# Operands' offsets in SBUF, the layout of the S5 kernel in memory, and the place of a root among GpSimd's tables

## The chip, the cores and the metric

The kernel runs on one core of a Trainium2 chip. The metric is the device time of one execution in microseconds. Inputs and outputs lie in DRAM; weights come as float32 and stay float32.

## The reference, cut to what matters

One decoder block on x of 512 tokens by 2048 channels:

```
mod = silu(c) @ w_ada + b_ada                 # 6 sections of 2048: sh1 sc1 ga1 sh2 sc2 ga2
h = rmsnorm(x, g) * (1 + sc1) + sh1
u, q, kc, vc, ks, vs, kw, vw, gl = split(h @ w_in)
y_ssm = S5(u)        # 64 groups of 16 channels, 64 complex states each; gelu and a gated 1024x1024 product
y_att = NSA(q, ...)  # 16 heads: compressed, selected and windowed attention, gated
x = x + ga1 * (concat(rmsnorm(y_ssm), rmsnorm(y_att)) @ w_out)
h = rmsnorm(x, g2) * (1 + sc2) + sh2
up = causal_conv3(h @ w_up) + conv_b          # 2048 -> 2 x 5632
x = x + ga2 * ((silu(gate) * val) @ w_down)
out = rmsnorm(x, g_final)
```

For S5, the states' decay `a = exp(lam * dt)` gives tables of powers of a for each group, with sines and cosines built by polynomials and angle doubling. S5 needs them, together with `f = (a - 1) / lam`.

## The kernel before

**Products.** Every float32 operand is split into a high part (a cast to a shorter float32, the type `fp32r` in the profile) on ScalarE (ACT) and a low part (source minus high part) on VectorE (DVE). `mm3` (L85 to L89) then makes three matmuls for each pair of tiles: wh·xh, wh·xl and wl·xh. In names such as `dn<-ah,wh` of the profile the first input (ah) streams through TensorE (PE) as the moving operand and the second (wh) is the 128x128 tile of weights. Each matmul loads its own weights.

**Stages**, in the order of time: phase A (0 to 240 us) makes the modulation and the first norm and projects u, k and v. Its first half multiplies by `wu` for u, its second half by `wk`. b1 (240 to 540) makes the 12 remaining projections and, between them, 8 octets of S5 (8 groups each), and ends with the gate and the compressed keys. b2 is attention with the gated product of S5 beside it, and c the output projection (together 540 to about 1033). Then the up projection (`up_first` for 2 of 44 channel blocks, `up_rest` for 42) until 1860, and the down projection until 2350, with the last norm behind it.

**Up projection.** `up_rest` makes each block by 7 products in place of 8 (a Strassen-like scheme): for 7 weight tiles (`a11`, `a12`, `a22`, and sums such as `a21 + a22`) and 7 operands of 256 columns that stand ready (`b11`, `b21`, `t4`, `t1`, `t2`, `b22`, `t3`, each with a part h and a part l). A product is 8 steps of `mm3`, so 24 matmuls of 256 columns, and a block is 168 matmuls. The split weights go in turn into the pair wh, wl of the pool `wp` and the pair xh, xl of the pool `pe` (L1167 to L1174), so that half of all products use each pair. `up_first` uses wh, wl and a pair rh, rl.

**Where the tiles lie.** Pools are opened like a stack from the left and, with `side="right"`, from the right of each partition's memory. A pad `rp` of 8 floats is the first on the right (L1314), and the tile `tapn` (with a pad to 48 x 3 floats, L1326) stands on the left ahead of everything opened after it. The pool `wp` stands ahead of both. The start addresses, modulo 128 bytes, of moving operand and weights are therefore, before the change:

```
matmuls                                        moving  weights
up, dn, mm (yh, yl), b1 and A with wh, wl        64       64
up with xh, xl and with rh, rl                   64        0
dn with wz (the last 96 of the down projection)  64        0
s<-K,Q (scores)                                   0        0
pv<-tl,Vs and pv<-th,Vs                          64        0
```

**First norm.** In phase A the sums of squares go through TensorE, DVE adds epsilon (`rms_v`, L131), GpSimd (POOL) takes the power -1/2 (`rms_r`, L133), and TensorE spreads the result (L136) for the scale `rb`, which the whole second half of phase A needs. GpSimd also computes the S5 tables (`s5_prep`, L325 to L481), in one instruction stream. The stream is written by a scheduler; `tc.high_priority(-100000)` puts the tables behind everything else, and a list `hold` binds two copies at the beginning of the second half of the tables to a place behind the root. Behind the tables stand the queue's DMA writes of k and v (`qk_d`, `v_d`).

**S5 in an octet** (L491 to L636). Tables of the octet on DVE (`s5C`, `s5S`, `s5bb`, `s5bg`, `s5TT`), weights `s5W` by transposes on TensorE, a product of `bb` and `TT` that gives the octet's convolution kernel `Kt` of 16 x 1024, its write to DRAM (`k_s`, L582), a read back as a banded 128 x 128 x 8 tile (`s5w3`, shown as `s5w` in the profile, L586), then states by a scan, and the output Y, to which 8 matmuls with `w3[:, :, g]` as weights (L631) and 8 with `TT` (L632) contribute. `Kt`, `k_s` and `w3` have the group index g innermost, so that the 128 weights of one group lie 32 bytes apart. Octets are issued in the loop over the projections (L706).

Of the kernel before, what the change touches and what calls it, by code (L numbers as in the profile page):

```python
# [18 lines left out]
P = 128  # L19
# [28 lines left out]
M_K, M_C = 0, 512  # L48
NM = 640


class Block:
# [88 lines left out]
    def setup(self):  # L141
# [3 lines left out]
        self.dp = ctx.enter_context(tc.tile_pool(name="dp", bufs=1, space=DRAM))  # L145
        cp = self.cp

        self.vecs = cp.tile([P, 176], F32, name="vecs")[:, 0:NV]
# [48 lines left out]
    def phase_a(self, hh, hl, tab, ps):  # L197
# [4 lines left out]
        with ExitStack() as st:  # L202
# [59 lines left out]
            for kt in range(KT):  # L262
# [12 lines left out]
                if kt == 1:  # L275

                    zero = pa.tile([P, P], F32, name="zero")
                    nc.gpsimd.memset(zero, 0.0)
                    self.after([nc.gpsimd.dma_start(
                        self.k_s.rearrange("o i x -> (o i) x")[:, 1024:].rearrange("p (a b) -> p a b", b=P),  # L280
                        zero.unsqueeze(1).to_broadcast([P, 7, P]))], first)
                if 2 <= kt < 10:
# [42 lines left out]
    def s5_prep(self, pool, W):  # L325
        nc, tc, V = self.nc, self.tc, self.nc.gpsimd
        sgn, nsgn = self.cst(C_SGN), self.cst(C_NSGN)
        vin = W.tile([P, 3, 64], F32, name="vin")
        nc.sync.dma_start(vin, self.a["s5v"])
        with tc.high_priority(-100000):  # L330
# [79 lines left out]

            for m in (1, 2, 4):
                cmul(PR[:, 8 - 2 * m:8 - m], PI[:, 8 - 2 * m:8 - m], PR[:, 8 - m:8], PI[:, 8 - m:8],
                     bc(PR[:, 8 - m], m), bc(PI[:, 8 - m], m), tmp[:, :m])
            ar, ai = PR[:, 7], PI[:, 7]
            den, q, rd, nr = t(), t(), t(), t()
# [30 lines left out]
            def powers(C, Sn, c, s):  # L446
                V.memset(C[:, 0], 1.0)
                V.memset(Sn[:, 0], 0.0)
                after = [V.tensor_copy(C[:, 1], c), V.tensor_copy(Sn[:, 1], s)]
                if hold:  # L450
                    self.after(after, hold.pop())
                cmul(C[:, 2], Sn[:, 2], C[:, 1], Sn[:, 1], C[:, 1], Sn[:, 1], tmp[:, 0])
                cmul(C[:, 3], Sn[:, 3], C[:, 2], Sn[:, 2], C[:, 1], Sn[:, 1], tmp[:, 0])
                ec, es = t(), t()
                cmul(ec, es, C[:, 2], Sn[:, 2], C[:, 2], Sn[:, 2], tmp[:, 0])
                cmul(C[:, 4:8], Sn[:, 4:8], C[:, 0:4], Sn[:, 0:4], bc(ec, 4), bc(es, 4), tmp[:, :4])
                return ec, es

        yield

        hold = [self.rms_pow]
        with tc.high_priority(-100000):
            ec, es = powers(CB, SB, c8, s8)
# [27 lines left out]
    def s5_octet(self, o, Tb, W, ps):  # L491
# [78 lines left out]
        Kt = W.tile([P, 8, 9 * 16], F32, name="s5bg", bufs=3).rearrange("p a b -> p (a b)")  # L570
        Kt = Kt[:16, 0:1024].rearrange("p (x g) -> p x g", g=8)
        with hp():
            for q in range(2):
                p = ps.tile([P, 4, P], F32, name="tp", bufs=2)
                for g in range(4):
                    T.matmul(p[:16, g], bb[:, 0, 4 * q + g], TT[:, 4 * q + g, 1:9].rearrange("p k h -> p (k h)"),
                             start=True, stop=True)
                A.copy(Kt[:, :, 4 * q:4 * q + 4].rearrange("p x g -> p g x"), p[:16])
        dd = W.tile([16, 16, 8], F32, name="s5dd")
        nc.sync.dma_start(dd, a["s5d"][:, o])  # L580
        V.tensor_add(Kt[:, 112:], Kt[:, 112:], dd)
        nc.gpsimd.dma_start(self.k_s[o, :, 0:1024].rearrange("i (x g) -> i x g", g=8), Kt)  # L582
        w3 = W.tile([P, P, 8], F32, name="s5w3")

        src = self.k_s[o]
        nc.gpsimd.dma_start(w3.rearrange("p x g -> p (x g)"),  # L586
                            bass.AP(src.tensor, src.offset, [[P, 8], [15 * P, 16], [1, 1024]]))

# [39 lines left out]
        with hp():  # L628
            Y = ps.tile([P, S], F32, name="acc", bufs=4)
            for g in range(8):  # L630
                T.matmul(Y[:, 64 * g:64 * g + 64], w3[:, :, g], U[:, g], start=True, stop=False)  # L631
                T.matmul(Y[:, 64 * g:64 * g + 64], TT[:, g, 0:8].rearrange("p k h -> p (k h)"), SS[:, g, 0:64],  # L632
                         start=False, stop=True)
            zz = W.tile([P, 8, 64], F32, name="s5x", bufs=4)
            A.activation(zz.rearrange("p g j -> p (g j)"), Y, AF.Gelu_apprx_tanh)
            nc.gpsimd.dma_start(self.z_d[o].rearrange("(h g) l j -> l h g j", g=8), zz)  # L636
# [24 lines left out]
    def phase_b1(self, hh, hl):  # L661
        nc, tc, a, V, A, T = self.nc, self.tc, self.a, self.V, self.A, self.T
        with ExitStack() as st:
# [17 lines left out]
            for i in range(12):  # L681
# [3 lines left out]
                with tc.high_priority():  # L685
# [13 lines left out]
                    else:  # L699
# [5 lines left out]
                        self.spill(self.qk_d[g, P * t:P * t + P], p, t2, -0.125)  # L705
                while 12 * n < 7 * (i + 1):  # L706
                    octet(n)
                    n += 1
# [602 lines left out]
    def run(self):  # L1311
        tc = self.tc
        self.setup()
        self.ctx.enter_context(tc.tile_pool(name="rp", bufs=1, side="right")).tile([P, 8], F32, name="pad")  # L1314
        sc = ExitStack()
# [9 lines left out]
        self.taps = ta.tile([P, 88, 4], F32, name="taps")  # L1325
        self.tapn = ta.tile([P, NFF + 4, 3], F32, name="tapn")[:, 0:NFF]  # L1326
        with ExitStack() as st:
# [163 lines left out]
```

## Time and profile before

| | |
|---|---|
| times of three runs, us | 2372.95, 2373.53, 2375.1 (median 2373.53) |
| the profiled execution, us | 2375.8, span 2374.0 |
| granted TensorE clock, mean over the span | 0.964 |
| busy share of the span: PE, DVE, ACT, POOL | 94%, 79%, 46%, 12% |

The span is the time from the first to the last recorded instruction. "Busy" counts the time in which an engine had an instruction; matmuls overlap, so a busy TensorE can still be at different paces, and the distance between starts tells the pace. A granted clock of 1.0 is 2.4 GHz, 0.5 is 1.2 GHz.

### The profile page before, as it was taken

Reading aid. Unit: us, or ns where it says so; the run is one execution under the profiler, and the core shown is the slowest. Engines: PE = TensorE matmul, PEld = TensorE weight load, DVE = VectorE, ACT = ScalarE, POOL = GpSimd, SP = SyncE. Lnnn points to the kernel's source line nnn. Section 1 sums busy time; section 2 is a strip of 40 time slices with the busy share of each in tenths; the row PEclk is TensorE's granted clock in tenths of the full one; section 3 lists DMA queues with packets and bytes.
Section 4 is the critical chain, followed back from the end, with each engine's and each line's share of the span. In section 5 each row is a group of like instructions: output and inputs, shape, how many; then the busy total and the mean of one; then the engine's idle time right before and its main releaser. Section 6 shows DMA issues by size and latency. Waiting matters only on the chain.

```text
span 2374.0 us, 34691 instructions
## 1 busy us (share of the span) xinstructions
PE 2223.8 (94%) x13694; PEld 1963.5 (83%) x13694; DVE 1864.5 (79%) x2776; ACT 1083.3 (46%) x1807; POOL 284.5 (12%) x375
## 2 busy tenths in 40 slices
PE   7779999988899889899999999999999899999997
PEld 5657787866677667889999999999999788888887
DVE  7789878749988878889999999999999686434436
ACT  4222535448867742644444444444444422222215
POOL 7996110100000001000000000000000000000000
PEclk9889989979999889999999999999999999999998
DMA  8666745676567568233333333333333585333323
GB/s 342 257 218 224 238 143 148 186 207 193 183 215 228 185 251 302 99 123 119 117 117 120 118 117 118 118 118 118 118 118 120 233 313 227 124 107 124 107 89 107
DMA packets 92370, 398.17 MB, mean 168 GB/s; under 512 B 19776, under 2 KB 28352, under 8 KB 56240
## 3 DMA queue, kind: packets, MB, share of 16 engines
q1 hardware_dynamic: 77856, 344.60, 41.7%
q0 software_dynamic: 14352, 51.36, 6.3%
q8 instruction: 107, 1.75, 0.3%
q14 instruction: 55, 0.45, 0.1%
HBM read 358.20 MB, written 37.69 MB: 167 GB/s over the span
## 4 chain that ended last, share of the span: by engine, by line
PE 71%; DVE 10%; issue 6%; POOL 5%; ACT 4%; DMA 3%; SPq 0%; POOLq 0%; DVEq 0%; ACTq 0%
PE dn L88 7%; PE dn L87 7%; PE dn L89 7%; PE sa L89 7%; PE sa L88 7%; PE sa L87 7%; PE sb L87 5%; PE sb L89 5%; PE sb L88 5%; PE mm L87 2%; PE mm L89 2%; PE mm L88 2%; POOL stt L339 2%; DVE wl L62 2%; PE s L871 1%
## 5 line engine op out<-in xcount | busy, mean ns | idle before, releaser
L62 ACT CAST wh<-wr 128x1024 fp32r<-128x1024 f32 (+1 forms) x257 | 262.1, 1025 | 508.7 <-PE dn L88 324.3
L62 DVE TENSOR_TENSOR wl<-wr,wh 128x1024 fp32r<-128x1024 f32 (+1 forms) x255 | 307.2, 1209 | 64.2 <-ACT wh L62 43.2
L87 PE MATMUL dn<-ah,wh 128*128 128x512 f32 (+1 forms) x704 | 271.3, 386 | 7.5 <-ACT ah L62 7.5
L88 PE MATMUL dn<-al,wh 128*128 128x512 f32 (+1 forms) x704 | 271.3, 386 | 0.0
L89 PE MATMUL dn<-ah,wl 128*128 128x512 f32 (+1 forms) x704 | 271.0, 385 | 0.0
L1250 DVE SCALAR_TENSOR_TENSOR x<-dn,mod,x 128x512 f32<-128x512 f32 (+1 forms) x104 | 73.3, 709 | 192.4 <-PE dn L89 191.9
L87 PEld LDWEIGHTS dn<-ah,wh 128*128 128x128 f32 x704 | 132.8, 189 | 34.3 <-ACT ah L62 7.7
L111 DVE SCALAR_TENSOR_TENSOR adw<-adw,silc 128x2048 f32<-128x2048 f32 x63 | 150.2, 2386 | 11.8 <-DMA adw<-in_wada_dram 11.8
L88 PEld LDWEIGHTS dn<-al,wh 128*128 128x128 f32 x704 | 132.6, 188 | 26.9 <-DVE al L62 0.7
L89 PEld LDWEIGHTS dn<-ah,wl 128*128 128x128 f32 x704 | 132.7, 188 | 26.2
L62 ACT CAST wh<-wq 128x1024 fp32r<-128x1024 f32 x84 | 88.1, 1050 | 137.6 <-DVE wq L1194 101.1
L62 ACT CAST xh<-wq 128x1024 fp32r<-128x1024 f32 x84 | 87.9, 1046 | 135.9 <-DVE wq L1194 100.7
L87 PE MATMUL mm<-yh,wh 128*128 128x512 f32 (+1 forms) x320 | 129.4, 409 | 21.4 <-ACT yh L62 6.2
L88 PE MATMUL mm<-yl,wh 128*128 128x512 f32 (+1 forms) x320 | 128.3, 401 | 3.7 <-DVE yl L62 3.7
L1083 POOL DMA_DIRECT2D a_d<-cv x44 | 23.8, 541 | 877.4 <-DVE cv L1082 877.4
L62 DVE TENSOR_TENSOR wl<-wq,wh 128x1024 fp32r<-128x1024 f32 x84 | 102.4, 1220 | 32.9 <-ACT wh L62 32.9
L89 PE MATMUL mm<-yh,wl 128*128 128x512 f32 (+1 forms) x320 | 127.4, 400 | 0.4 <-DVE wl L62 0.4
L62 DVE TENSOR_TENSOR xl<-wq,xh 128x1024 fp32r<-128x1024 f32 x84 | 102.6, 1221 | 31.5 <-ACT xh L62 31.5
L1194 DVE TENSOR_TENSOR wq<-wq,wr 128x1024 f32<-128x1024 f32 x84 | 102.2, 1216 | 0.1
L87 PEld LDWEIGHTS mm<-yh,wh 128*128 128x128 f32 x320 | 63.0, 199 | 36.1 <-issue 11.6
L87 PE MATMUL b<-hh,wh 128*128 128x512 f32 x192 | 68.8, 416 | 23.5 <-ACT hh L239 14.7
L62 ACT CAST xh<-wr 128x1024 fp32r<-128x1024 f32 x63 | 65.8, 1045 | 44.8 <-PE sa L88 31.6
(525 smaller groups left out, 7210.5 us busy)
## 6 DMA issues: line engine op xcount, KB each, us to landing
adw<-in_wada_dram SPq DMA_DIRECT2D x49, 1024.0 KB, 6.7
wr<-in_wup_dram SPq DMA_DIRECT2D x46, 1024.0 KB, 4.9
wq<-in_wup_dram SPq DMA_DIRECT2D x42, 1024.0 KB, 6.8
wr<-in_wdn_dram SPq DMA_DIRECT2D x40, 1024.0 KB, 4.9
wr<-in_wada_dram SPq DMA_DIRECT2D x32, 1024.0 KB, 4.9
wr<-in_wout_dram SPq DMA_DIRECT2D x16, 1024.0 KB, 5.4
adw<-in_wada_dram POOLq DMA_DIRECT2D x14, 1024.0 KB, 6.9
wr<-in_wp_dram SPq DMA_DIRECT2D x12, 1024.0 KB, 5.3
```

The costliest lines, as they stand in the source:

```text
L62: return self.A.copy(hi, src), self.V.tensor_sub(lo, src, hi.bitcast(F32))
L87: self.T.matmul(ps, wh, xh, start=start, stop=False)
L88: self.T.matmul(ps, wh, xl, start=False, stop=False)
L89: self.T.matmul(ps, wl, xh, start=False, stop=stop)
L111: self.V.scalar_tensor_tensor(t, t, 1.0, self.silc, op0=ALU.mult, op1=ALU.mult, accum_out=out)
L339: V.tensor_scalar(w, x, c, None, op0=op0)
L871: T.matmul(s[:, :c + n], q[hd], K[b][:, i, k0:k0 + c + n], start=i == 0, stop=i == 1)
L1083: self.nc.gpsimd.dma_start(self.a_d[:, m], val)
L1194: V.tensor_add(src, src, add)
L1250: V.scalar_tensor_tensor(x, p, self.mod[:, 5, m:m + 1], x, op0=ALU.mult, op1=ALU.add)
```

## The change

It has four parts.

1. The pad `rp` grows from 8 to 24 floats, and `tapn` takes 160 floats in place of 144. Every tile on the right moves by 64 bytes modulo 128, and so does every tile on the left that is opened after `tapn`. The addresses are then: up, dn and mm with wh, wl: moving 0, weights 64. Up with xh, xl and rh, rl, and dn with wz: moving 0, weights 64. Scores 64, 64. pv with th, tl: 0, 64. Phase A and b1 stay at 64, 64.
2. The S5 kernel lies by group: `Kt`, `k_s` and `w3` have the group outermost, and `w3[:, g]` is contiguous. Rows of `k_s` are 8 pieces of 240 floats (128 of data, 112 zeros). Its write becomes 128 pieces of 512 bytes for each octet (16 of 4 KB before), its read 1024 pieces of 512 bytes (128 of 4 KB before).
3. The load of `vin`, from which the tables start, moves from the queue of SP to the head of GpSimd's. The first part of the tables ends after the first squaring, and everything from `square(2)` on is held behind the root.
4. Octets are issued by `12 * n < 8 * (i - 1)` in place of `12 * n < 7 * (i + 1)`.

```diff
+class Held:
+    def __init__(self, engine, hold):
+        self.engine, self.hold = engine, hold
+    def __getattr__(self, name):
+        def issue(*args, **kw):
+            i = getattr(self.engine, name)(*args, **kw)
+            self.hold(i)
+            return i
+        return issue
...
-                    zero = pa.tile([P, P], F32, name="zero")
+                    zero = pa.tile([P, 112], F32, name="zero")
...
-                        self.k_s.rearrange("o i x -> (o i) x")[:, 1024:].rearrange("p (a b) -> p a b", b=P),
-                        zero.unsqueeze(1).to_broadcast([P, 7, P]))], first)
+                        self.k_s.rearrange("o i (g x) -> (o i) g x", g=8)[:, :, P:],
+                        zero.unsqueeze(1).to_broadcast([P, 8, 112]))], first)
...
-        nc.sync.dma_start(vin, self.a["s5v"])
+        nc.gpsimd.dma_start(vin, self.a["s5v"])
...
-            for m in (1, 2, 4):
+            def square(m):
                 cmul(PR[:, 8 - 2 * m:8 - m], PI[:, 8 - 2 * m:8 - m], PR[:, 8 - m:8], PI[:, 8 - m:8],
                      bc(PR[:, 8 - m], m), bc(PI[:, 8 - m], m), tmp[:, :m])
+            square(1)
+        yield
+        V = Held(V, lambda i: self.after([i], self.rms_pow))
+        with tc.high_priority(-100000):
+            square(2)
+            square(4)
...
-                after = [V.tensor_copy(C[:, 1], c), V.tensor_copy(Sn[:, 1], s)]
-                if hold:
-                    self.after(after, hold.pop())
+                V.tensor_copy(C[:, 1], c)
+                V.tensor_copy(Sn[:, 1], s)
...
-        yield
-        hold = [self.rms_pow]
-        with tc.high_priority(-100000):
...
-        Kt = Kt[:16, 0:1024].rearrange("p (x g) -> p x g", g=8)
+        Kt = Kt[:16, 0:1024].rearrange("p (g x) -> p g x", g=8)
...
-                A.copy(Kt[:, :, 4 * q:4 * q + 4].rearrange("p x g -> p g x"), p[:16])
+                A.copy(Kt[:, 4 * q:4 * q + 4], p[:16])
...
-        nc.gpsimd.dma_start(self.k_s[o, :, 0:1024].rearrange("i (x g) -> i x g", g=8), Kt)
-        w3 = W.tile([P, P, 8], F32, name="s5w3")
+        nc.gpsimd.dma_start(self.k_s[o].rearrange("i (g x) -> i g x", g=8)[:, :, 0:P], Kt)
+        w3 = W.tile([P, 8, P], F32, name="s5w3")
...
-                            bass.AP(src.tensor, src.offset, [[P, 8], [15 * P, 16], [1, 1024]]))
+        nc.gpsimd.dma_start(w3, bass.AP(src.tensor, src.offset, [[16, 8], [15 * P, 16], [15 * 16, 8], [1, P]]))
...
-                T.matmul(Y[:, 64 * g:64 * g + 64], w3[:, :, g], U[:, g], start=True, stop=False)
+                T.matmul(Y[:, 64 * g:64 * g + 64], w3[:, g], U[:, g], start=True, stop=False)
...
-                while 12 * n < 7 * (i + 1):
+                while 12 * n < 8 * (i - 1):
...
-        self.ctx.enter_context(tc.tile_pool(name="rp", bufs=1, side="right")).tile([P, 8], F32, name="pad")
+        self.ctx.enter_context(tc.tile_pool(name="rp", bufs=1, side="right")).tile([P, 24], F32, name="pad")
...
-        self.tapn = ta.tile([P, NFF + 4, 3], F32, name="tapn")[:, 0:NFF]
+        self.tapn = ta.tile([P, 160], F32, name="tapn")[:, 0:3 * NFF].rearrange("p (c j) -> p c j", j=3)
```

The order of GpSimd's instructions around the root, of the kernel before (L133 is the root; `sp` and `stt` are temporaries of the tables, `s5CB` and `s5SB` tables of cosines and sines):

```order
L383 TENSOR_SCALAR dw<-sp_392 128x64
L339 TENSOR_SCALAR stt<-sp_391 128x64
L340 TENSOR_TENSOR sp_401<-stt,dw 128x64
L339 TENSOR_SCALAR stt<-sp_391 128x64
L340 TENSOR_TENSOR sp_402<-stt,sp_391 128x64
L444 TENSOR_SCALAR sp_416<-sp_402 128x64
L279 DMA k_s<-zero 128x7x128
L133 TENSOR_TENSOR rms_r<-rms_v,mhalf 128x4
L449 COPY s5CB<-sp_416 128x64
L449 COPY s5SB<-sp_401 128x64
L401 TENSOR_TENSOR s5CB<-s5CB 128x64
```

And of the changed kernel (its line numbers are higher by 13 to 17; L146 is the root, and a held instruction has L59, the line of the wrapper):

```order
L418 TENSOR_TENSOR s5PI<-s5PR,s5PI 128x64
L417 TENSOR_TENSOR s5PR<-s5PR,sp_331 128x64
L419 TENSOR_TENSOR sp_331<-s5PI,s5PR 128x64
L420 TENSOR_TENSOR s5PI<-s5PI,sp_331 128x64
L293 DMA k_s<-zero 1024x1x112
L146 TENSOR_TENSOR rms_r<-rms_v,mhalf 128x4
L59 TENSOR_TENSOR s5PR<-s5PR 128x128
L59 TENSOR_TENSOR sp_331<-s5PI 128x128
L59 TENSOR_TENSOR s5PI<-s5PR,s5PI 128x128
```

The root stood at place 154 of GpSimd's order and now stands at 107. 48 instructions that stood ahead of it are behind it now, and the load of `vin` came in ahead.

The end of the tables on GpSimd before:

```order
L476 TENSOR_SCALAR sp_413<-sp_413,cons 128x512
L479 COPY s5CH<-sp_412 64x256
L478 COPY s5SH<-sp_413 64x256
L479 COPY s5SH<-sp_413 64x256
L659 DMA qk_d<-adw 128x1024 x2
L305 DMA v_d<-adw 128x512
L659 DMA qk_d<-adw 128x1024 x2
L305 DMA v_d<-adw 128x512 x3
```

and now:

```order
L59 COPY s5CH<-sp_1059 64x256
L59 COPY s5SH<-sp_1060 64x256 x2
L59 TENSOR_TENSOR s5fr<-s5fr,sp_1005 128x64
L59 TENSOR_TENSOR s5fi<-s5fi,sp_1005 128x64
L59 TENSOR_SCALAR s5fi<-s5fi,cons 128x64
L675 DMA qk_d<-adw 128x1024 x2
L319 DMA v_d<-adw 128x512
L675 DMA qk_d<-adw 128x1024 x2
L319 DMA v_d<-adw 128x512 x3
```

The DMA writes of k and v stand right behind the last table in both; what stands ahead of the tables' end is longer by the instructions that were moved.

On TensorE, ACT, DVE and SP the order of b1 is the same, but for the reciprocal of the tables on DVE (from place 11 to the middle of phase A's second half) and for octets 6 and 7. The front of octet 6 on TensorE before, between the matmuls of a projection (`mm<-hh`) and ahead of the output of octet 5 (`acc<-s5U,s5w`):

```order
L568 MATMUL tp<-cons,s5bg 128x128 x8
L88 MATMUL mm<-hl_1512,wh 128x512
L89 MATMUL mm<-hh_106,wl 128x512
L87 MATMUL mm<-hh_108,wh 128x512
L88 MATMUL mm<-hl_1553,wh 128x512
L89 MATMUL mm<-hh_108,wl 128x512
L87 MATMUL mm<-hh_110,wh 128x512
L88 MATMUL mm<-hl_1594,wh 128x512
L622 MATMUL acc<-s5x,cons 128x512
L631 MATMUL acc<-s5U,s5w_3262 128x64
L89 MATMUL mm<-hh_110,wl 128x512
L576 MATMUL tp<-s5TT,s5bb 16x128 x8
```

and now, in the projection that follows the output of octet 5:

```order
L102 MATMUL mm<-hh_94,wl 128x512
L100 MATMUL mm<-hh_96,wh 128x512
L101 MATMUL mm<-hl_97,wh 128x512
L796 MATMUL tp<-qt 128x124
L585 MATMUL tp<-cons,s5bg 128x128 x4
L102 MATMUL mm<-hh_96,wl 128x512
L100 MATMUL mm<-hh_98,wh 128x512
L101 MATMUL mm<-hl_99,wh 128x512
L618 MATMUL acc<-bg,cons 128x8
L585 MATMUL tp<-cons,s5bg 128x128
L593 MATMUL tp<-s5TT,s5bb 16x128 x3
L625 MATMUL acc<-s5U,s5W_3600 128x64 x2
```

Transposes (`tp<-cons,s5bg`) and kernel products (`tp<-s5TT,s5bb`) of octet 6 moved behind the whole output of octet 5, and stand now among the sums of the octet's own input (`acc<-s5U,s5W`).

## Rows read from the trace of the kernel before

**Rows 1.** Busy time of the engines by stage. Columns: stretch in us, length, and for PE, PE's weight loads (PEld), DVE, ACT and POOL the busy us and in brackets the instructions; then the granted clock, the share of DMA and GB/s.

```profile
0.00:103.00 103.00, 88.25 (x379) 71.22 (x380) 85.42 (x112) 41.25 (x49) 84.63 (x101) 1.00 0.90 341
103.00:128.00 25.00, 3.21 (x13) 2.68 (x13) 2.37 (x3) 1.07 (x2) 24.20 (x63) 0.54 0.12 38
128.00:240.00 112.00, 99.03 (x397) 78.34 (x397) 103.78 (x104) 30.88 (x39) 86.58 (x67) 0.94 0.69 230
240.00:540.00 300.00, 282.74 (x1389) 233.02 (x1387) 224.40 (x419) 142.90 (x305) 31.29 (x47) 0.93 0.62 185
540.00:1120.00 580.00, 517.45 (x2980) 432.90 (x2981) 501.54 (x1061) 363.39 (x820) 35.33 (x58) 0.94 0.55 189
1120.00:1860.00 740.00, 739.84 (x6249) 732.71 (x6248) 677.77 (x745) 356.50 (x411) 19.97 (x37) 1.00 0.33 118
1860.00:2350.00 490.00, 482.50 (x2216) 402.62 (x2215) 254.59 (x307) 140.09 (x172) 1.08 (x2) 0.99 0.44 162
```

**Rows 2.** DVE's instructions in order of time, around the first norm. Columns: start us, length us, engine, line, operation, tiles and shapes; in square brackets the idle time before it and what ended it.

```profile
103.08 0.16 DVE L131 TENSOR_SCALAR rms_v<-b 128x4 f32<-128x4 f32 x1 [1.10 <-PE b L129]
...
128.14 0.94 DVE L310 SCALAR_TENSOR_TENSOR modt<-x,mod,rb 128x512 f32<-128x512 f32 x1 [22.69 <-ACT rb L258]
```

**Rows 3.** GpSimd's instructions in order of time (columns as in rows 2): the first table row, the last of the first squaring, and the root.

```profile
12.61 0.65 POOL L348 TENSOR_SCALAR ex<-vin 128x64 f32<-128x64 f32 x1 [11.16 <-DMA vin<-in_s5v_dram]
...
110.38 0.32 POOL L406 TENSOR_TENSOR s5PI<-s5PI,sp 128x64 f32<-128x64 f32 x1
...
123.04 1.22 POOL L279 DMA_DIRECT2D k_s<-zero  x1
124.29 1.06 POOL L133 TENSOR_TENSOR rms_r<-rms_v,mhalf 128x4 f32<-128x4 f32 x1
```

**Rows 4.** GpSimd's groups by line and shape from 105 to 123 us, where DVE is idle. Columns: line, operation, tiles, shapes, count, then busy us and mean ns, then idle us.

```profile
L340 POOL TENSOR_TENSOR sp<-stt,sp 128x64 f32<-128x64 f32 x4 | 1.3, 316 | 0.2
...
L403 POOL TENSOR_TENSOR s5PR<-s5PR,sp 128x256 f32<-128x256 f32 x1 | 0.7, 719 | 0.0
```

**Rows 5.** The same from 128 to 217 us, where DVE is busy.

```profile
L403 POOL TENSOR_TENSOR sp<-sp,sp 128x64 f32<-128x64 f32 x5 | 5.7, 1150 | 0.2
...
L403 POOL TENSOR_TENSOR s5CB<-s5CB,sp 128x256 f32<-128x256 f32 x1 | 2.8, 2789 | 0.0
```

**Rows 6.** GpSimd in order of time: the last tables and the first writes of k.

```profile
207.55 2.24 POOL L475 TENSOR_TENSOR sp<-sp,sp 128x512 f32<-128x512 f32 x1
...
215.18 0.89 POOL L479 COPY s5SH<-sp 64x256 f32<-64x256 f32 x1
239.25 0.68 POOL L659 DMA_DIRECT2D qk_d<-adw  x1 [23.18 <-DVE adw L62]
```

**Rows 7.** DVE in order of time at octet 0: the first uses of the tables, and the low part of the weights for the next projection.

```profile
243.54 0.62 DVE L546 TENSOR_TENSOR s5C<-s5CH,s5CB 128x256 f32<-128x256 f32 x1
...
244.58 0.62 DVE L547 TENSOR_TENSOR s5x<-s5SH,s5SB 128x256 f32<-128x256 f32 x1 [0.42 <-DMA qk_d<-adw]
...
246.56 1.22 DVE L62 TENSOR_TENSOR wl<-wr,wh 128x1024 fp32r<-128x1024 f32 x1
```

**Rows 8.** Weight loads on TensorE from 240 to 545 us, by line and shape: the strided `s5w` and contiguous ones. A float32 matmul loads its weights twice, so 128 loads are 64 matmuls.

```profile
L631 PEld LDWEIGHTS acc<-s5U,s5w 128*128 128x128 f32 x128 | 36.0, 323 | 3.5 <-issue 2.7
L632 PEld LDWEIGHTS acc<-s5SS,s5TT 128*128 128x128 f32 x128 | 21.3, 204 | 1.1 <-DVE s5SS L627 0.9
```

**Rows 9.** DMA issues: size of one and the median us from issue to landing.

```profile
s5w<-k_s POOLq DMA_DIRECT2D x8, 512.0 KB, 7.6
...
z_d<-s5x POOLq DMA_DIRECT2D x8, 256.0 KB, 6.3
```

**Rows 10.** All instructions with the tile `s5w`. Columns: line, engine, operation, tiles, count, then ns min/median/max, then the start of the first and the last in us.

```profile
L631 PEld LDWEIGHTS acc<-s5U,s5w x128: 312/314/338, 291.6 to 507.3; 128*128 128x128 f32 x128
...
L586 POOL DMA_DIRECT2D s5w<-k_s x8: 612/724/825, 277.4 to 479.8; - x8
```

**Rows 11.** TensorE in order of time in `up_rest`: the first matmul of three products that follow one another, each of 24 matmuls.

```profile
1399.27 0.28 PE L87 MATMUL sa<-t1h,xh 128*128 128x256 f32 x1
...
1401.99 0.28 PE L87 MATMUL sb<-t2h,wh 128*128 128x256 f32 x1
...
1404.87 0.28 PE L87 MATMUL sa<-b22h,xh 128*128 128x256 f32 x1
```

**Rows 12.** TensorE's groups in the down projection (1875 to 2350 us) by line and shape, those of 256 columns.

```profile
L88 PE MATMUL dn<-al,wh 128*128 128x256 f32 x25 | 7.1, 283 | 0.0
L89 PE MATMUL dn<-ah,wz 128*128 128x256 f32 x16 | 4.4, 276 | 0.0
```

**Rows 13.** TensorE in order of time in the down projection: the first and the ninth of 9 matmuls of 512 columns.

```profile
1999.72 0.39 PE L89 MATMUL dn<-ah,wl 128*128 128x512 f32 x1
...
2001.53 0.39 PE L88 MATMUL dn<-al,wh 128*128 128x512 f32 x1
```

**Rows 14.** TensorE in order of time in attention: the first and the fourth of 4 matmuls of 512 columns.

```profile
772.84 0.39 PE L907 MATMUL pv<-tl,Vs 128*64 128x512 f32 x1
...
773.52 0.39 PE L908 MATMUL pv<-th,Vs 128*128 128x512 f32 x1
```

**Rows 15.** TensorE in order of time in attention: two score matmuls of 256 columns and what follows them.

```profile
714.97 0.40 PE L871 MATMUL s<-K,Q 128*128 128x256 f32 x2
715.22 0.39 PE L88 MATMUL mm<-yl,wh 128*128 128x512 f32 x1
```

More of the change, by code (lines that the diff above doesn't have):

```diff
@@ L577, in s5_octet @@
                              start=True, stop=True)
-                A.copy(Kt[:, :, 4 * q:4 * q + 4].rearrange("p x g -> p g x"), p[:16])
+                A.copy(Kt[:, 4 * q:4 * q + 4], p[:16])
         dd = W.tile([16, 16, 8], F32, name="s5dd")
         nc.sync.dma_start(dd, a["s5d"][:, o])
-        V.tensor_add(Kt[:, 112:], Kt[:, 112:], dd)
-        nc.gpsimd.dma_start(self.k_s[o, :, 0:1024].rearrange("i (x g) -> i x g", g=8), Kt)
-        w3 = W.tile([P, P, 8], F32, name="s5w3")
+        V.tensor_add(Kt[:, :, 112:], Kt[:, :, 112:], dd.rearrange("p x g -> p g x"))
+        nc.gpsimd.dma_start(self.k_s[o].rearrange("i (g x) -> i g x", g=8)[:, :, 0:P], Kt)
+        w3 = W.tile([P, 8, P], F32, name="s5w3")
         src = self.k_s[o]
-        nc.gpsimd.dma_start(w3.rearrange("p x g -> p (x g)"),
-                            bass.AP(src.tensor, src.offset, [[P, 8], [15 * P, 16], [1, 1024]]))
+        nc.gpsimd.dma_start(w3, bass.AP(src.tensor, src.offset, [[16, 8], [15 * P, 16], [15 * 16, 8], [1, P]]))
         bu = W.tile([P, 2], F32, name="bu", bufs=2)
```

## The prediction

> **What bounds the kernel now.** I read the table by stage first [rows 1]. From 1120 to 1860 us TensorE is busy for 739.84 of 740 us at full clock, and DVE for 677.77: the up projection is set by the pace of its matmuls. In the down projection TensorE has 482.50 of 490 and DVE half. In b1 (240 to 540) TensorE has 282.74 of 300, DVE 224.40. So in these three stages a matmul that becomes shorter is worth nearly its saving. The odd stretch is 103 to 128: all engines but GpSimd stand still (TensorE 3.21 of 25 us).
>
> The order of time on DVE tells why [rows 2]: epsilon is added at 103.08, and a later instruction starts at 128.14 after 22.69 us of idling, released by the scale `rb`. On GpSimd [rows 3] the root, ready since 103.24, begins at 124.29, because the tables stand ahead of it. So about 22 us there are one wait for a queue.
>
> **Part 3, root and tables.** First the root's new time. The last row of the first squaring began at 110.38 [rows 3]; now only `k_s<-zero` (1.22 us) stands between it and the root. The tables began at 12.61, when `vin` had landed, after 11.16 us of idling; with the load at the head of GpSimd's queue and a flight of some 4 us I put the start at 5, so 7.6 earlier. Some held rows among those before 110.38 go too (about 2 us), but those that ran while DVE stood still now meet a busy DVE: a row of 64 columns takes 316 ns beside an idle DVE [rows 4] and 1150 beside a busy one [rows 5], which gives back some 3 us. 110.7 - 7.6 - 2 + 3 + 1.2 = 105, end 106, against 125.35. The second half of phase A so starts some 19 us earlier: the stall shrinks from 22 us to 3.
>
> Second, what is late next: the tables. 76 instructions stood behind the root and took 125.3 to 216.1 [rows 3, 6]; now there are 48 more by the order: 32 of 64 columns, 4 memsets, 6 of 128 and 6 of 256 columns. Beside a busy DVE I take 1.0, 0.2, 1.5 and 2.2 us (somewhat under the 1150 and 2789 ns of [rows 5], since not every row meets DVE), together 55. From 106 that makes 106 + 55 + 91 = 252. DVE reaches its first table use, L546, at 243.54 [rows 7], now 19 earlier, at 224.5, and stops. The last 27.5 us then run beside an idle DVE; by the rows of 512 columns (2.24 [rows 6] against about 1.4, twice the 719 ns of 256 columns [rows 4]) this is some 15 us. The tables end near 239.5. Behind them stand the writes of k, first issued at 239.25 before [rows 6], for which DVE's next instruction L547 waits until 244.58 [rows 7]. Now they are issued at 239.5, and L547 comes at about the same time as before. Behind it in DVE's order is the low part of the next projection's weights, made at 246.56 to 247.78 [rows 7]. TensorE's projection 0 moves up by the 19 us and is done long before; it waits there for some 16. So of 19 us saved about 3 are left at the end, and a restart after a long wait costs: behind the stall of before the granted clock of the stretch was 0.54 [rows 1]. I take -1.5 us. The load of `vin` itself costs nothing: GpSimd idled then for 11.16 us [rows 3], and SP's queue loses an issue. The reciprocal of the tables, now among DVE's rows of the second half, uses a sum that stands 10 rows behind the root; DVE comes to it some 40 us later, so it waits for nothing. If the tables ran that late, DVE's whole queue would stand behind it. Bounds: -19 (the tables end in time), +6 (the tables end 9 us later than worked out).
>
> **Part 2, the S5 kernel by group.** A strided weight load takes 323 ns, contiguous ones of the same shape 204 [rows 8]. 128 loads x (323 - 204) = 15.2 us over the octets, on an engine that is busy 94% of b1 [rows 1]. Against it: the read of 512 KB now consists of 1024 pieces of 512 bytes. Before it landed in 7.6 us; `z_d`, 1024 pieces of 256 bytes, in 6.3 [rows 9]. I expect 7 to 12, and the first read was issued at 277.4 for a first use at 291.6 [rows 10], so nothing; without that lead the output would wait for up to the 5 us more. ACT's copies of `Kt` and DVE's sum change only their strides, on engines with idle time in b1 [rows 1]. Part 4 leaves TensorE's order alone up to octet 6; there the front moves behind the output of octet 5, so the last two octets have fewer projection matmuls to hide DVE's tables. I take +4 for this, and -11 for parts 2 and 4 together; bounds 0 (the tail eats it all) and -24 (with some of the clock regained that b1 lacks, granted 0.93 [rows 1]).
>
> **Part 1, 64 bytes.** In `up_rest` all matmuls have one shape, and two weight pairs take turns. 24 matmuls with xh, xl take 1401.99 - 1399.27 = 2.72 us (113.3 ns each), the next 24 with wh, wl 1404.87 - 1401.99 = 2.88 (120.0) [rows 11]. The same in the down projection: 283 and 276 ns for wh and wz [rows 12]. By the table of addresses, the slow pair lies at the moving operand's address modulo 128, the fast one 64 bytes from it. After the change all up products are 64 apart, with the roles turned round (moving 0, weights 64), which no row shows. I take the distance as what matters: 42 blocks x 84 slow matmuls x 6.67 ns = 23.5 us, and 192 in `up_first`, 1.3. DVE with 678 of 740 us [rows 1] still has room when a block falls from 19.6 to 19.0 us.
>
> For 512 columns the down projection has 8 distances in 1.81 us, 226 ns, at distance 0 [rows 13]; pv, 64 apart, has 3 in 0.68, 227 [rows 14]. So I take nothing for the 2016 matmuls of 512 columns in the down projection and 864 of the output products. The bound is 6.67 ns each, -13.4 and -5.8. The 288 of 256 columns there give -1.9. Scores stay at distance 0.
>
> A rule speaks against this part. The Trainium skill, page "SBUF — State Buffer", section "Who interferes with whom", gives TensorE two read ports for the moving operand and for weights, independent of each other, and says that it never waits on anyone. By that rule alone the sum would lose all 26.7 us of part 1, and the time be 2361. The trace does not agree with it as it stands: 113.3 and 120.0 ns for one shape [rows 11]. It could be kept if the address of the weights alone decides, which is a rival.
>
> **Sum.** -1.5 - 11 - 24.8 - 1.9 = -39.2. From the profiled 2375.8 this is 2336.6. That execution lies 2.3 us above the median of 2373.53, so 2334.
>
> **Rivals.**
> - *512 columns gain too.* Both widths lose time at the weight load, which is equally long for either. For it: 226 ns is 13 more than 512 columns at 2.4 GHz need, as 120 is 13 more than 256 need. Against it pv's 227 [rows 14]. 2334 - 19 = 2315. Chance 17%.
> - *The stall's gain is kept.* The tables end by 224, as their rows are slowed less than I take. Against it the 2.8 us of [rows 5]. 2334 - 17 = 2317. 8%.
> - *The offset does nothing for up* (something else differs between the pairs, as the pool). 2334 + 26.7 = 2361. 8%.
> - *The tables end after 247, and b1 gains nothing,* because DVE's late work sets its end. 2334 + 6.5 + 1 + 11, about 2352. 5%.
> - *The slower one: the weights' own address decides.* Weights at 0 modulo 128 would be the quick ones, and all move to 64. Then xh, xl, rh, rl and wz fall to 120 ns: 3528 x 6.67 = 23.5, + 1.3 + 0.6 = +25.4, with -12.5 of parts 2 to 4: 2373.5 + 12.9 = 2386. It decides as soon as it outweighs 12.5 us, that is from about half of its price. For it: no row has moving 0 and weights 64. Against it: scores, with both at 0, take 0.25 us for two of 256 columns [rows 15], 125 each, not 113. 12%.
>
> **How the numbers follow.** The forecast, 2318 to 2350 on its own, has 50%. The range for 8 in 10 reaches from 2300 (the first two rivals in part together) to 2364 (the third inside); it leaves out the slower one and a few per cent at each end. A measurement of this kernel can tell 0.2% (4.7 us) from no change. Faster than that: forecast 50, the first two 25, most of the third and fourth 11, less a little for gains that cancel: 84%. Same: 5%. Slower: 11%, nearly all of the last.
>
> **What would show it.** In the profile after: a root soon after 105 us with a stall of about 3; L546 of octet 0 waiting for GpSimd for some 15 us, and TensorE idle ahead of projection 1; weight loads of `s5w` near 200 ns; 2.72 us for 24 matmuls in `up_rest` whichever pair, at full clock, and a stage that is 23 us shorter; 226 ns still in the down projection. I am wrong in direction if 24 matmuls take 2.88 us for both pairs, and in size if 512 columns fall to 220 ns or the tables hold nobody up.

## The result and the profile after

The changed kernel takes 2357.75 us in the median of 4 runs (2354.28 to 2360.18), the kernel before 2373.24 beside it: a ratio of 0.9932, 95% interval 0.9915 to 0.995. That is 15.5 us (12 to 20 by the interval), where 39 were forecast. The direction was right, the range held the time, and the size was wrong by more than half.

By stage, in the columns of [rows 1]:

```profile
103.00:128.00 25.00, 21.32 (x90) 16.90 (x90) 20.86 (x22) 8.69 (x13) 24.32 (x23) 0.93 0.66 198
128.00:240.00 112.00, 88.96 (x374) 70.57 (x373) 87.30 (x104) 31.89 (x41) 105.46 (x114) 0.92 0.67 233
240.00:540.00 300.00, 265.76 (x1395) 213.59 (x1394) 229.22 (x449) 135.64 (x313) 32.50 (x38) 0.93 0.64 181
540.00:1120.00 580.00, 513.73 (x2994) 428.25 (x2993) 497.53 (x1028) 357.96 (x804) 35.65 (x59) 0.94 0.54 187
```

Fixed windows mislead here, as the stages have moved. More is seen in the start of the first matmul of each stage, taken from the profiles of all kernels of this study. For the kernel before it is the time in us from the span's start, for the others the difference from it; "S5" is the first and the last matmul with `s5w` as weights.

```
                     norm  proj 0  S5 first  S5 last  scores  pv last  up_rest    down     end
before              125.4   239.6     292.0    507.3   512.5    855.2   1025.5  1875.8  2374.0
changed             -18.7   -29.2     -10.9    -15.1   -18.9    -11.2     -5.6   -28.9   -15.6
e1 offsets            0.8     0.1       0.5      2.0     1.9     -3.5     -4.3   -28.0   -15.4
e2 root             -18.7   -28.7     -12.4    -11.3   -11.4    -14.6    -15.7   -16.3   -15.0
e3 by group           0.2    -1.0       0.1    -20.8   -21.5    -23.8    -21.0   -20.8   -20.9
e4 octets             0.2     0.1      -0.2      9.8     6.1      8.3      6.9     7.4     6.9
e8 all but octets   -18.7   -29.3     -11.1    -32.6   -33.3    -32.1    -29.3   -53.0   -40.2
e10 all but offsets -18.8   -27.7     -11.3    -17.5   -21.3    -19.5    -16.7   -17.1   -16.9
e9 offset for up    -18.9   -29.2     -10.8    -31.2   -31.5    -35.0    -32.0   -55.6   -55.9
e6 weights at 0       0.4     1.0       1.4     -0.4    -0.5      0.5     -3.8   -27.0   -14.8
e11 writes of k     -18.8   -29.8     -20.7    -42.0   -31.8    -35.6    -37.4   -59.7   -58.7
e12 octets earlier  -18.3   -28.9      -8.6    -25.8    -5.7    -13.0    -15.2   -38.6   -39.0
e13 vin on SP       -14.4   -22.8      -6.9    -28.8   -29.0    -30.2    -27.6   -50.9   -51.1
e14 e11+e12         -18.9   -29.5     -20.9    -33.1   -12.4    -21.0    -20.7   -43.8   -44.2
```

The line of the changed kernel tells the story: 29 us ahead at projection 0, 11 at the first octet; 19 at the scores, 6 at `up_rest`; 29 again at the down projection, and 16 at the end. So something is given back in three places.

**The stall.** GpSimd and DVE in order of time (columns as in [rows 2]); they answer to [rows 2, 3, 6, 7]:

```profile
103.69 3.01 POOL L146 TENSOR_TENSOR rms_r<-rms_v,mhalf 128x4 f32<-128x4 f32 x1 [1.48 <-DVE rms_v L144]
231.50 1.21 POOL L675 DMA_DIRECT2D qk_d<-adw  x2
```

```profile
109.38 1.06 DVE L324 SCALAR_TENSOR_TENSOR modt<-x,mod,rb 128x512 f32<-128x512 f32 x1 [3.58 <-ACT rb L272]
229.94 0.61 DVE L563 TENSOR_TENSOR s5C<-s5CH,s5CB 128x256 f32<-128x256 f32 x1 [13.29 <-POOL s5SH L59]
236.17 0.60 DVE L564 TENSOR_TENSOR s5x<-s5SH,s5SB 128x256 f32<-128x256 f32 x1 [5.62 <-DMA qk_d<-adw]
238.03 1.24 DVE L75 TENSOR_TENSOR wl<-wr,wh 128x1024 fp32r<-128x1024 f32 x1
```

The root now waits 1.48 us for epsilon, where it stood behind the tables for 21 us before; DVE's idle time falls from 22.69 us to 3.58. The wait comes back at octet 0: 13.29 us for the tables and 5.62 for the writes of k behind them.

**TensorE's own waits** from 205 to 500 us, the longest (who waited for whom: us in total, times, longest):

```profile
PE mm L102 <- DVE wl L75: 17.5, 1, 17.5
PE acc L647 <- DMA s5w<-k_s: 7.3, 1, 7.3
```

The first is the price of the tables. The second is new: the output of the seventh octet (octet 6 of the order lists) waits for its kernel to come back from DRAM. The read of that kernel and its first use, in the changed kernel and then in e8 below, which differs from it by part 4 alone:

```profile
444.39 1.33 POOL L603 DMA_DIRECT2D s5w<-k_s  x1 [6.25 <-PE tp L585]
452.58 0.69 PE L647 MATMUL acc<-s5U,s5w 128*128 128x64 f32 x2 [7.29 <-DMA s5w<-k_s]
```

```profile
419.32 1.37 POOL L603 DMA_DIRECT2D s5w<-k_s  x1
440.40 0.33 PE L647 MATMUL acc<-s5U,s5w 128*128 128x64 f32 x2
```

With part 4 the read is issued at 444.39 us and TensorE is ready for it at 445.3, so it waits; without part 4 the read is issued 21 us ahead of its use. Two stretches of the changed kernel, the second half of phase A and the one around that wait, in the columns of [rows 1]:

```profile
106.70:210.30 103.60, 97.10 (x404) 77.15 (x405) 95.69 (x105) 31.35 (x38) 101.44 (x103) 0.97 0.74 249
443.20:497.40 54.20, 37.69 (x202) 29.27 (x200) 22.31 (x48) 17.70 (x39) 6.33 (x6) 0.80 0.63 135
```

The kernel before has this for the first of them:

```profile
125.40:239.60 114.20, 101.23 (x405) 80.51 (x406) 103.78 (x104) 30.96 (x39) 88.77 (x77) 0.92 0.69 228
```

The same work takes 10.6 us less, with 8.1 us less busy time of DVE and a granted clock of 0.97 in place of 0.92. In the stretch around the wait TensorE is busy for 37.69 of 54.20 us, at 0.80.

**Pace.** In `up_rest` 24 matmuls take 2.72 us now with either pair: 1397.20 - 1394.48 below, with xh and xl, and the median distance between starts with wh, wl is 113 ns too, against 120 in [rows 11]. In the down projection 8 distances are 1.87 us, 234 ns, against 1.81 in [rows 13].

```profile
1394.48 0.28 PE L100 MATMUL sb<-b11h,xh 128*128 128x256 f32 x1
...
1397.20 0.28 PE L100 MATMUL sa<-t4h,xh 128*128 128x256 f32 x1
```

```profile
1999.61 0.39 PE L100 MATMUL dn<-ah,wh 128*128 128x512 f32 x1
...
2001.48 0.39 PE L102 MATMUL dn<-ah,wl 128*128 128x512 f32 x1
```

So the offset sped up the matmuls of 256 columns and slowed those of 512.

### The profile page after: what moved, and what is told of

The parts are those of the page before. It is cut to its first block, busy times and chain, and to the rows that moved or that the text cites. A ratio compares the mean times of both kernels' runs of the same rounds, so it can differ in the third digit from the quotient of the medians.

```text
span 2358.4 us, 34686 instructions
## 1 busy us (share of the span) xinstructions
PE 2195.3 (93%) x13694; PEld 1917.5 (81%) x13694; DVE 1856.5 (79%) x2776; ACT 1074.7 (46%) x1807; POOL 310.3 (13%) x376
## 3 DMA queue, kind: packets, MB, share of 16 engines
HBM read 358.20 MB, written 37.69 MB: 168 GB/s over the span
## 4 chain that ended last, share of the span: by engine, by line
PE 57%; issue 4%; DVE 1%; ACT 1%; POOL 1%; DMA 1%; POOLq 0%; DVEq 0%; ACTq 0%
PE sa L102 7%; PE sa L100 7%; PE sa L101 7%; PE dn L100 7%; PE dn L101 7%; PE dn L102 7%; PE sb L100 5%; PE sb L102 5%; PE sb L101 5%; DMA adw<-in_wada_dram 0%; POOL adw L119 0%; DMA ar<-a_d 0%; POOL x_d L1045 0%; PE mm L100 0%; PE mm L101 0%
## 5 line engine op out<-in xcount | busy, mean ns | idle before, releaser
L75 ACT CAST wh<-wr 128x1024 fp32r<-128x1024 f32 (+1 forms) x257 | 262.0, 1024 | 521.9 <-PE dn L101 331.6
L146 POOL TENSOR_TENSOR rms_r<-rms_v,mhalf 128x2 f32<-128x2 f32 (+1 forms) x8 | 10.8, 1345 | 648.0 <-DVE rms_v L144 647.9
L102 PE MATMUL mm<-hh,wl 128*128 128x512 f32 x192 | 78.8, 411 | 17.5 <-DVE wl L75 17.5
```

The costliest lines, as they stand in the source:

```text
L75: return self.A.copy(hi, src), self.V.tensor_sub(lo, src, hi.bitcast(F32))
L102: self.T.matmul(ps, wl, xh, start=False, stop=stop)
L146: self.rms_pow = self.nc.gpsimd.tensor_tensor(r[:, 0:n], v[:, 0:n], self.mhalf.to_broadcast([P, n]), op=ALU.pow)
```

## The experiments

Runs of later groups were compared with the kernel before on the same chip, where it took 2378.6 to 2381.3 us in the median. The ratios are the measure, with their 95% intervals in brackets; a ratio is turned into us with the 2373.5 of the first runs.

**e1: the offsets alone.**

```diff
-  "rp" ... tile([P, 8])            -  tapn = tile([P, NFF + 4, 3])
+  "rp" ... tile([P, 24])           +  tapn = tile([P, 160])
```

> The kernel before with part 1 alone (both pads). Theory W (width): with moving operand and weights 64 bytes apart, matmuls of 256 columns take 113 ns (120 before), and those of 512 columns become slower, 231 to 236 ns (227 before). Then the up projection is some 23 us shorter, the down projection some 13 longer, the output products (864 of 512 columns) 4 to 6 longer: about 2368 in all, -4 to -8. Rival: the slower matmuls of 512 columns come from another part of the change (the octets' order or the tables have no way to do this in the down projection, but the clock might); then the down projection stays at 227 ns and the time is about 2348.

Measured: 0.9942 (0.9922 to 0.9963). The up projection is 23.7 us shorter (-4.3 to -28.0 in the table), the down projection 13 longer, with a median distance of 235 ns between its matmuls of 512 columns (227 before; half of them lie between 231 and 236). Theory W holds for both widths. The rival falls: nothing else was changed, TensorE's order is the same, and the granted clock is 1.00 in both runs, while 1832 matmuls are counted in 415 us of the down projection before and 1781 here (columns of [rows 1]):

```profile
1885.00:2300.00 415.00, 415.00 (x1832) 343.41 (x1831) 207.70 (x238) 102.44 (x113) 0.00 (x0) 1.00 0.46 167
```

```profile
1885.00:2300.00 415.00, 415.00 (x1781) 334.36 (x1780) 200.13 (x231) 98.28 (x110) 0.00 (x0) 1.00 0.41 146
```

The time was off all the same: 14 us under before (9 to 18), where 4 to 8 were expected. The 4 to 6 us that the output products were to lose do not show: from the scores to `up_rest` this run gains 6, and no run tells why.

**e6: both apart with the roles turned round.** Only wh and wl move, by 64 bytes (a larger `wr` ahead of them, a pad behind).

```diff
-  raw = self.wp.tile([P, 2080], ...)   +  raw = self.wp.tile([P, 2088], ...)
+  self.wpad = self.wp.tile([P, 16], F32, name="wpad")   # behind the first wl
```

> The kernel before, with only the tiles wh and wl moved by 64 bytes: all up products have the moving operand at 64 and the weights at 0 modulo 128, and so have phase A, b1, the output products and the down projection. Theory W1: being 64 apart is what makes 512 columns slow, whichever of the two lies at 0. Then 256 columns take 113 ns, and 512 columns 231 to 236 everywhere, in phase A and b1 too (some 3000 matmuls more than 4 ns longer): up -23 us, down +13, the rest +4 to +8, in all -6 to 0. Rival W2: only the role, weights at 64 with the moving operand at 0, is slow at 512 columns. Then 512 columns stay at 227 here, or fall to 220, and the time is 23 us under before, or up to 45. Rival W3: the weights' or the operand's pool matters and not the address; then nothing changes.

Measured: 0.9951 (0.993 to 0.9972). All products of the up projection run at 113 ns, and the down projection is again slow:

```profile
1999.76 0.39 PE L89 MATMUL dn<-ah,wl 128*128 128x512 f32 x1
...
2001.16 0.39 PE L89 MATMUL dn<-ah,wl 128*128 128x512 f32 x1
```

These are 6 distances in 1.40 us, 233 ns. Which of the two operands lies at 0 does not matter for either width: W1 holds in its mechanism, W2 and W3 fall. Its time was off: 12 us under before (7 to 17), where 0 to 6 were expected. The matmuls of phase A and b1, now 64 apart too, have medians of 226 to 234 ns by group (226 or 227 before), but these stages lose no more than 1.4 us at any mark of the table: what slower matmuls cost there is not seen.

**e2: the root and the tables alone** (parts 1, 2 and 4 undone in the changed kernel).

> The kernel before with part 3 alone (root among the tables, load of vin on GpSimd's queue). Theory W says nothing on it. Theory Q (queue): the root starts at about 104, the second half of phase A starts 19 us earlier, DVE waits 13 us for the tables and 5 more for the writes of k behind them, TensorE waits 17, and 11 us of the 19 are left at the first output of an octet and at the end: about 2362. Rival 1: all 19 are kept or more, 2354. Rival 2: what is left is lost again in b1 and in attention, since other engines set their pace: 2370 to 2374.

Measured: 0.9945 (0.9928 to 0.9963), 13 us. The lead at the norm is 18.7, at the first octet 12.4, and it stays between 11 and 16 to the end. DVE waits 12.7 us for the tables and 5.6 for the writes of k, TensorE 15.9. Theory Q holds; neither rival does.

**e13: `vin` back on SP's queue,** in the version e9 below.

```diff
-  nc.gpsimd.dma_start(vin, self.a["s5v"])   +  nc.sync.dma_start(vin, self.a["s5v"])
```

> The same version with the load of vin back on SP's queue; GpSimd's order is otherwise the same. Theory Q: the tables start 7 us later, the root is ready at about 108 to 110 in place of 104, and the tables end some 5 to 7 us later too, which TensorE's wait ahead of projection 1 passes on: 5 to 7 us more than with the load on GpSimd, a ratio near 0.980. Rival: GpSimd's rows wait for DVE anyway and the start does not matter: no change.

Measured: 0.9772 (0.9747 to 0.9797), against 0.9774 (0.975 to 0.9798) for e9: not told apart. In its trace the root starts later, TensorE's wait at projection 1 is shorter (15.2 in place of 17.7), and the end is 4.8 us later than in e9's:

```profile
109.81 1.11 POOL L146 TENSOR_TENSOR rms_r<-rms_v,mhalf 128x4 f32<-128x4 f32 x1
```

The mechanism is there in the trace, but the runs' spread hides 5 us: the intervals allow either sign, and what the load's move is worth stays open.

**e11: the writes of k on SP's queue,** in e9.

```diff
-  self.nc.gpsimd.dma_start(dst, t)              # spill, end of phase A
+  (eng or self.nc.gpsimd).dma_start(dst, t)     # eng = nc.sync there
```

> The version with parts 2 and 3, the old issue of octets and the offset for the up projection alone (-53.8 us by its ratio, 0.9774), with the writes of k at the end of phase A on SP's queue in place of GpSimd's. Theory Q: these writes no longer stand behind the tables, DVE's second table instruction starts right behind the first (5.6 us after it in the changed kernel), and TensorE's wait of 17.5 us ahead of projection 1 falls to about 12: some 5 us less, a ratio near 0.975. Rival: SP's queue, which holds the loads of weights, then waits for the writes' data, or the first output of octet 0 is late for another reason; then 0 to 5 us more.

Measured: 0.9718 (0.969 to 0.9746), the best time of the study (median 2312.15). DVE's second table instruction follows the first at once:

```profile
229.37 0.60 DVE L563 TENSOR_TENSOR s5C<-s5CH,s5CB 128x256 f32<-128x256 f32 x1 [13.29 <-POOL s5SH L59]
229.89 0.73 DVE L564 TENSOR_TENSOR s5x<-s5SH,s5SB 128x256 f32<-128x256 f32 x1
```

TensorE's wait at projection 1 fell from 17.7 to 12.1 us. Theory Q holds in kind. The octets gain more than the 5 us (20.7 ahead at the first, 10.8 in e9), but this run is not the queue alone: the order on TensorE and SP changed with it, and 158 projection matmuls stand ahead of the first octet's output in place of 167. Most of that goes again ahead of the scores (8.0 us of waiting for `K<-qk_d`). By the intervals the gain on e9 lies between 1 and 26 us; the profiles' ends differ by 2.8. That it is faster is shown, by little; how much, and how much of it the queue gives, is not.

**e3: the S5 kernel by group alone.**

```diff
-  w3 = W.tile([P, P, 8]); w3[:, :, g]; Kt "p (x g) -> p x g"
+  w3 = W.tile([P, 8, P]); w3[:, g];    Kt "p (g x) -> p g x"   # and k_s to match
```

> The kernel before with part 2 alone (S5 kernel by group). Theory L (weight load): the loads of s5w fall from 323 to about 200 ns, TensorE sets the pace of b1, so nearly all of 15 us is gained: about 2360. Rival: in b1 DVE or the DMA of 512-byte pieces sets the pace of the octets, and 0 to 6 us are gained: 2367 to 2374, with the same weight loads.

Measured: 0.9927 (0.9902 to 0.9951), 17 us. The weight loads, in the columns of [rows 8], are as short as the others:

```profile
L630 PEld LDWEIGHTS acc<-s5U,s5w 128*128 128x128 f32 x128 | 20.3, 194 | 4.4 <-issue 4.4
L631 PEld LDWEIGHTS acc<-s5SS,s5TT 128*128 128x128 f32 x128 | 19.8, 192 | 1.4 <-DVE s5SS L626 1.1
```

Theory L holds, with somewhat more than the 15.2 us of the loads (the interval reaches from 12 to 23).

**e4: the later issue of octets alone.**

```diff
-  while 12 * n < 7 * (i + 1):   +  while 12 * n < 8 * (i - 1):
```

> The kernel before with part 4 alone (octets issued later). Theory T (tail): the octets before the sixth run as before, the last two lose the cover of the projections, and b1's end and the first tenth of attention come 5 to 10 us later: 2378 to 2384. Rival: the later issue only reorders work under TensorE's matmuls, within 2 us of before: 2372 to 2376.

Measured: 1.0035 (1.0018 to 1.0051), 8 us slower; theory T holds, the rival does not. The seventh octet's output waits for its kernel here too, which lies in pieces of 4 KB in this run, so the pieces are not the cause:

```profile
PE acc L631 <- DMA s5w<-k_s: 6.1, 1, 6.1
```

**e8: the changed kernel with the old issue of octets.**

> The changed kernel with the old issue of octets (parts 1, 2 and 3). The parts alone gave -13.7, -13.1 and -17.4 us by their ratios and part 4 +8.3, which is -36 together, while the change gave -16. Theory O (octets): part 4 is what costs, more beside the others than alone; without it the time is 40 to 45 us under before. Rival P: the parts overlap, since b1 and attention are then paced by other engines, and the time stays within 6 us of the changed kernel's 16 under before. In between: the 8 us of part 4 alone come back, -24.

Measured: 0.9826 (0.9802 to 0.9849). Against 0.9932 this is 0.0106, or 25 us for part 4 beside the others (16 to 35 by the intervals). Its profile has no wait for `s5w` at all; the octets' outputs begin at 440.4 and 466.0 us in place of 452.6 and 483.5, after times equal to 0.4 us up to 55% of the projections. By the table 14 of the 25 us are there at the scores, 7.3 of them in the one wait; 9 more come between the scores and `up_rest`, and their cause was not traced. Theory O holds, P falls: parts 1 to 3 add up (-13.7, -13.1, -17.4 alone make -44; -41 together).

**e10: the changed kernel without the offsets.**

> The changed kernel without part 1 (parts 2, 3 and 4). Theory O: part 4 eats what parts 2 and 3 give, so with -13.1, -17.4 and +8.3 alone the three together give less than 22 us, about 5 to 15 under before, and attention starts some 20 us earlier but ends only 11 earlier. Rival P2: the loss in attention came from the shifted tiles of attention (scores at 64, pv at 0 and 64); then these three add up, 22 us under before, and attention keeps its lead.

Measured: 0.9937 (0.9916 to 0.9957). Parts 2, 3 and 4 give 15 us, where 2 and 3 alone sum to 30. The lead falls from 21 to 17 between the scores and `up_rest` with attention's tiles where they were, so theory O holds. P2 gets no support, though the changed kernel loses 13 there and this one 5; what the other 8 are is open (e8, with the same tiles moved as the changed kernel, loses 4).

**e9: offset for the up projection alone, octets as before.**

```diff
-  "rp" ... tile([P, 24])   +  "rp" ... tile([P, 8])
+  R.tile([P, 16], F32, name="ptpad")     # behind the up projection's operands
...                                        # octets as in e8; tapn stays at 160 floats
```

> As the run before it in this group (parts 2 and 3, old issue of octets), with the operands 64 bytes apart in the up projection alone: the right side keeps its 8 floats of pad, and a pad stands behind the operands of the up projection. Theory W: the down projection is back at 227 ns and 13 us shorter, the output products 4 to 6 shorter, the up projection as short as with both pads: 15 to 20 us under the run before it, some 2.5% under before if theory O holds. Rival: the down projection stays at 231 to 236 ns, as its cause is not the address, and both runs agree.

The "run before it" is e8.

Measured: 0.9774 (0.975 to 0.9798), 12 us less than e8, where 15 to 20 were expected. TensorE's order is that of e8. The down projection is back at 226 ns:

```profile
1999.81 0.39 PE L102 MATMUL dn<-ah,wl 128*128 128x512 f32 x1
...
2001.17 0.39 PE L102 MATMUL dn<-ah,wl 128*128 128x512 f32 x1
```

6 distances make 1.36 us, where e6 has 1.40. The up projection kept its gain. Theory W holds, the rival falls. As `tapn` keeps its larger size, the 96 products with `wz` lie at distance 0 now and take 120 ns, 113 before.

**e12: octets issued earlier than in the kernel before,** in e9.

```diff
-  while 12 * n < 7 * (i + 1):   +  while n < 8 and 12 * n < 8 * (i + 1):
```

> The same version with octets issued earlier than in the kernel before (8(i+1) in place of 7(i+1)), so that the seventh and eighth move up by some ten matmuls of a projection. Theory T (cover): what part 4 took by moving them back is a matter of degree, and moving them forward gives 2 to 8 us at the end of b1: a ratio of 0.974 to 0.977. Rival: the old issue already has all the cover that these octets need; no change, or some us more since the projections then stand alone at the end.

Measured: 0.9815 (0.9793 to 0.9837), 10 us slower than e9 by the ratios, whose intervals just overlap. A miss: an earlier issue gives nothing. The last outputs come later, not earlier (474.8 us for the eighth octet, 467.4 in e9), and TensorE has other waits (440 to 560 us):

```profile
PE acc L638 <- DVE s5x L635: 8.3, 1, 8.3
PE s L888 <- DMA K<-qk_d: 5.7, 2, 5.0
```

Of the three issues tried the old one is the best by the ratios. With either of the others TensorE stands still for one step of an octet: 7.3 us for the kernel in the changed one, 8.3 for DVE's `s5x` here, with the projections' last 17 matmuls behind it in its queue.

**e14: e11 and e12 together.**

> The same version with both the writes of k on SP's queue and the earlier issue of octets. If theories Q and T hold, the sum of the two: 7 to 13 us less, a ratio near 0.973. If one of the rivals holds, its run alone tells which, and this one equals the other.

Measured: 0.9794 (0.9776 to 0.9813). The two do not add up. Against e11 the earlier issue costs 18 us, and here the intervals lie apart, so that it is slower is shown by this pair; the same wait for `s5x` stands in its trace, 8.6 us. Against e12 the writes of k are worth 5 us by the ratios, whose intervals overlap.

## Why the prediction was right and wrong

- *Part 1, 256 columns:* right. "The distance is what matters" was shown with both roles (e1, e6), and the 23.5 us for `up_rest` measured 23.7. The 1.3 for `up_first` did not show, and the 1.9 for the shorter matmuls of the down and output projections came only in part: in the changed kernel those of the down projection have a median of 118 ns, not 113. The slower rival falls: its order (moving 0, weights 64) is the changed kernel's own, and takes 113 ns.
- *Part 1, 512 columns:* a step that failed. "I take nothing for the 2016 matmuls of 512 columns" had a bound on the side of a gain only, 0 to -13.4. Measured: +13 us in the down projection (2016 matmuls x 6.5 ns). The four matmuls of pv [rows 14], at 227 ns, were read as the price of being 64 apart. They were not typical: of the 160 distances behind a pv matmul in the same trace 10 are 227 ns or less, and the median behind `pv<-th` is 233. Nor could attention have priced the offset, as products at distance 0 there (`mm<-yh,wh`) have a median of 232. e1 shows 235 for long runs of matmuls 64 apart. A bound below nothing, as the 6.67 ns of the other width with its sign turned, would have held it.
- *Part 4:* the other step that failed, and the larger. "I take +4" had no row under it; it measured +8 alone and +25 beside the others. What was read from the order was less cover for DVE's tables. What waited was TensorE, for the kernel's way to DRAM and back, 7.3 us, in a stretch in which it was busy for 37.69 of 54.20 us, at a granted clock of 0.80. That is a part of the 25; the 9 us between the scores and `up_rest` stay open. Parts 2 and 4 together, put at -11 with a bound of 0, so cost about 8 (-17 and +25).
- *Part 2:* the 15.2 us of the loads were right (17 measured alone). The DMA's lead, 14 us at the first octet, was taken for all octets; behind part 4 the seventh read is issued 0.9 us before TensorE is ready for it, and 7.3 us are waited. The prediction had named the price of a lost lead, up to 5 us, and not asked whether part 4 takes it away.
- *Part 3:* right in mechanism, wrong in size. Root at 103.69 (105 forecast), TensorE's wait 17.5 us (16). But "L547 comes at about the same time as before" failed: it came at 236.17, 8 us sooner, and 11 to 13 us of the stall were kept, not 1.5. The second half of phase A took 103.6 us in place of 114.2, so DVE was idle from 216.6, not 224.5, and the tables ended at 231.5, not 239.5. (By its own rows, 1.4 us in place of 2.24, the last 27.5 us of tables would have shrunk to 17, not 15; this is not what missed.) That DVE was slowed before by GpSimd's wide rows, of which the last now run in its idle time, is a reading of its 8.1 us less busy time, and was not tested; nor was what the clock's 0.97 had in it.

The terms that failed cancel in part: the forecast was 13 and 21 us too good in two of them and 12 too bad in the stall, which leaves 22 of the 24 us between forecast and result. That the time still fell into the wide range is owed to this, and so to luck.

The rule weighed there, of the Trainium skill, page "SBUF — State Buffer", section "Who interferes with whom", that TensorE's two read ports are independent and it never waits on anyone, does not agree with these runs if it is read as saying that the operands' places cannot matter: 113 and 120 ns, 227 and 235, by a shift of 64 bytes alone (e1, e6). What happens at the ports no run shows.

## What to carry to other kernels

An offset that speeds up one shape has to be priced for every shape that moves with it, with a bound on both sides; here a pad for one stage gained 24 us there and lost 13 in the next, and a pad local to the stage kept the gain. A price has to be read from all rows of its kind in the trace and not from four of them. When a long stall is taken out of one queue, look for the next user of that queue's results and for what is queued behind them. A DMA's lead read at one step of a loop holds for the others only as long as their order does.

## What was not expected of the hardware

The sign of the 64-byte offset turns with the width: at a granted clock of 1.00, 64 bytes apart in place of 0 takes 256 columns from 120 to 113 ns and 512 from 227 to between 231 and 236, and the same with the roles exchanged. No reason for the turn was found. In the down projection of e1 the short matmuls, of 256 columns with wh, have a median of 113 ns beside the long ones at 235, from the same pools of operands and weights, so it is the width that decides there. The 113 is not fixed: at the same addresses modulo 128 these short matmuls have a median of 118 in the changed kernel and 113 in e8, which is open too.
